# First product of the experts with weights stationary and tokens moving, rooms by rank, w1 and w3 in one array laid out by blocks

## The chip, the cores and the metric

The kernel runs on one core of one Trainium2 chip. The core has a matrix engine (TensorE: PE, with its weight loads shown apart as PEld), a vector engine (DVE), a scalar engine (ACT), a general engine (GpSimd: POOL) and SyncE (SP), which here only issues DMAs. The metric is device time in microseconds (us), the lower the better. All values are f32. Nearly every product is made of three: each operand is split into a rounded part "hi" and a rest "lo" (both of the type fp32r), and hi*hi + hi*lo + lo*hi is summed in PSUM.

## What is computed

One block of a network on 2048 tokens of width 1024: attention and a short convolution, then a mixture of experts, then a gated addition. The change lies in the experts (32 of them, in 4 groups of 8; every token goes to 2 experts of one group):

```python
def hier_moe(xn, w_group, b_group, w_router, b_router, w1, w3, w2):
    t, d = xn.shape                                        # 2048, 1024
    gl = (xn @ w_group).astype(jnp.float32) + b_group
    grp = jnp.argmax(gl, axis=-1)
    ...
    top_l, top_i = lax.top_k(el, TOP_K)                    # 2 of the 8 of the group
    wgt = (p_grp * jax.nn.softmax(top_l, axis=-1)).reshape(-1)
    eid = (grp[:, None] * EXPERTS_PER_GROUP + top_i).reshape(-1).astype(jnp.int32)
    ...
    def expert_block(args):
        xb, e = args
        hdn = jax.nn.silu(xb @ w1[e]) * (xb @ w3[e])       # 1024 -> 512
        return hdn @ w2[e]                                 # 512 -> 1024
```

The 4096 (token, expert) pairs are spread unevenly: by the reference's own routing of its inputs the 32 experts get, from the fullest to the emptiest, 177, 176, 171, 156, 152, 149, 149, 147, 146, 145, 145, 137, 137, 132, 132, 131, 129, 127, 120, 115, 113, 112, 112, 110, 108, 102, 102, 101, 94, 91, 91 and 87 rows.

## The kernel before

The program has four stages that follow each other: attention (`stage1`), convolution, gates and routing (`stage2`), the experts (`stage3`) and the gated addition (`stage4`). At the end of stage 2 `sort` ranks the experts by their rows, and writes for each rank the list of its tokens (`gidx` to gather, `sidx` to scatter) and the expert's number (`order`).

In `stage3` every expert has a room of fixed size: 192 rows for the 18 fullest (`NBIG`), 128 for the other 14. Rows over the room would go to a loop at the end (`overflow`); none is over here. The experts are taken in the order `proc`, in which large and small ones are mixed. For each one:

- `fetch` gathers the tokens' rows by an indirect DMA on POOL (part A: 128 rows, tile xgA; part B: 64 rows, xgB), two experts ahead. `prep` turns them on PE (lines L1008 and L1017) and splits them into xAh and xAl (ACT L1011, DVE L1012) and xB, in which hi and lo of the 64 rows stand side by side as 128 columns (L1019, L1020).
- `gemm1` multiplies with w1 and then w3: the tokens are stationary (128 x 128), the weights move with 512 columns at a time. For each of 8 pieces of the inner dimension part A takes three matmuls (`mm3`, L90 to L92), part B two (`mmB`, L1039 and L1040).
- Silu on ACT (L1073, L1077), the product of both on DVE (L1079) for A and on POOL (L1083) for B, where `fold` (L1045, L1046) has first added the hi rows to the lo rows.
- `turn_act` turns the result on PE (L1089, L1098) and splits it again into aAh, aAl and aB.
- `gemm2` multiplies with w2 (stationary: the turned result; moving: weights of 512 columns), copies to yA and yB and scatters them on POOL (L1106).

On PE the order is gemm1 of expert n, prep of n+1, gemm2 of n-1. Weights come in 384 chunks of 128 x 1024 f32 (512 KB): per expert four of w1, four of w3, four of w2. `chunk` takes the next one and asks `prefetch` for the one four further on. SP loads it into wraw (5 buffers), ACT makes whi (L79), and DVE or POOL make wlo (L80); whi and wlo have 7 buffers. POOL takes every fourth chunk, DVE the rest. Each engine works its instructions off in the order that the build's scheduler gave them. Results of matmuls go to 8 PSUM banks in turn.

The inner statements of the first product are:

```python
mm = self.mm3(pa, [(hi[:, k], lo[:, k])], [(ch[0][:, sl], ch[1][:, sl])], k, 8)
if xb is not None:
    mmB(pb, xb[:, k].rearrange("p s c -> p (s c)"), ch, sl, k == 0, k == 7)
```

## Time and profile before

| | us |
|---|---|
| median of 3 runs | 2657.95 |
| lowest and highest run | 2656.11, 2661.72 |
| the profiled execution, its own time | 2661.26 |
| its span (first to last instruction) | 2659.4 |
| expert stage in it, first transpose to last matmul of w2 (read off the timeline) | about 1627 to 2427 |

The page of the profile gives the busy time of each engine; the view by windows gives it for a stretch, with the granted clock of PE (1.00 is 2.4 GHz), the busy share of the DMA engines and what they moved. A matmul's record is longer than the time that it holds PE, since its end is modelled and the next one starts before it; so what one costs in a dense row is read from start to start. Names are those of the program: `acc<-whi,xAh` is a matmul into a PSUM bank, moving operand first, stationary operand behind it. In the view by line a row has the count, the busy time, the mean length of one and the idle time just before.

### The profile page before, as it was taken

The page shows a single profiled execution, that of the slowest core. Times are in us where ns is not written, and L with a number is a line of the kernel's source. Part 1 is how long each engine was busy: PE and PEld are TensorE (multiplying, and loading weights), DVE is VectorE, ACT ScalarE, POOL GpSimd, SP SyncE. Part 2 cuts the span into 40 slices and gives each one's busy share as a digit, 9 for nine tenths or more (in the row PEclk, how much of TensorE's full clock was granted, in tenths as well). Part 3 has the DMA queues.
Part 4 walks back from the last instruction along what each step waited for, and adds up shares of the span by engine and source line. Part 5 has one row for each costly group of instructions (what it writes and reads, how often), then busy time and mean ns, then how long its engine had stood idle before and what let it go on. Part 6 is the DMA issues. An engine that isn't in the chain of part 4 may idle for free.

```text
span 2659.4 us, 36515 instructions
## 1 busy us (share of the span) xinstructions
PE 2595.2 (98%) x13313; PEld 2184.5 (82%) x13313; DVE 1675.8 (63%) x2399; ACT 1341.6 (50%) x2025; POOL 841.0 (32%) x681
## 2 busy tenths in 40 slices
PE   7999999999999999999999998999999999998999
PEld 6898888878888888888888886888888888886887
DVE  7778867775444445444445446777777678775654
ACT  5666755564333323332333224766666666665322
POOL 2655465510000100010001003544554555542222
PEclk9999999999999999999999998999999999998999
DMA  5222311044335334533453346888989889987553
GB/s 185 72 68 60 110 48 41 9 129 137 102 128 189 103 95 143 170 102 95 137 170 103 95 151 210 307 309 295 315 304 313 302 314 309 312 309 258 207 187 103
DMA packets 349623, 465.11 MB, mean 175 GB/s; under 512 B 26240, under 2 KB 222080, under 8 KB 349440
## 3 DMA queue, kind: packets, MB, share of 16 engines
q1 hardware_dynamic: 314944, 388.35, 44.8%
q0 software_dynamic: 12096, 43.00, 4.3%
q10 hardware_dynamic: 22400, 31.41, 3.5%
q8 instruction: 105, 1.72, 0.3%
q14 instruction: 78, 0.64, 0.1%
HBM read 400.30 MB, written 62.39 MB: 174 GB/s over the span
## 4 chain that ended last, share of the span: by engine, by line
PE 84%; DVE 6%; DMA 4%; issue 3%; POOL 1%; ACT 1%; SPq 0%; another core or an unknown queue 0%; DVEq 0%; POOLq 0%; ACTq 0%
PE acc L90 22%; PE acc L92 22%; PE acc L91 22%; PE acc L1039 4%; PE acc L1040 4%; PE big L348 2%; PE big L380 2%; DMA h<-H 1%; DMA wraw<-w 1%; PE acc L393 1%; PE acc L394 1%; PE acc L1008 1%; PE acc L674 1%; PE acc L294 1%; POOL g L1362 1%
## 5 line engine op out<-in xcount | busy, mean ns | idle before, releaser
L80 DVE TENSOR_TENSOR wlo<-wraw,whi 128x1024 fp32r<-128x1024 f32 x464 | 694.5, 1509 | 478.4 <-ACT whi L79 465.3
L79 ACT CAST whi<-wraw 128x1024 fp32r<-128x1024 f32 x560 | 585.8, 1053 | 777.8 <-PE acc L91 375.6
L90 PE MATMUL acc<-nh,whi 128*128 128x512 f32 x896 | 349.7, 392 | 2.0 <-ACT nh L79 2.0
L91 PE MATMUL acc<-nl,whi 128*128 128x512 f32 x896 | 350.0, 391 | 0.0
L92 PE MATMUL acc<-nh,wlo 128*128 128x512 f32 x896 | 348.8, 389 | 0.0
L80 POOL TENSOR_TENSOR wlo<-wraw,whi 128x1024 fp32r<-128x1024 f32 x96 | 238.1, 2480 | 123.4 <-ACT whi L79 115.8
L599 POOL TENSOR_TENSOR sa<-sa,sc 128x512 f32<-128x512 f32 x32 | 41.3, 1290 | 538.3 <-DVE sc L598 493.2
L90 PE MATMUL acc<-whi,xAh 128*128 128x512 f32 x512 | 204.1, 399 | 0.4 <-ACT xAh L1011 0.4
L91 PE MATMUL acc<-wlo,xAh 128*128 128x512 f32 x512 | 200.1, 391 | 0.0
L92 PE MATMUL acc<-whi,xAl 128*128 128x512 f32 x512 | 200.0, 391 | 0.0
L90 PEld LDWEIGHTS acc<-nh,whi 128*128 128x128 f32 x896 | 168.1, 188 | 37.2 <-ACT nh L79 2.7
L92 PEld LDWEIGHTS acc<-nh,wlo 128*128 128x128 f32 x896 | 168.3, 188 | 34.5
L91 PEld LDWEIGHTS acc<-nl,whi 128*128 128x128 f32 x896 | 168.3, 188 | 33.4
L90 PE MATMUL acc<-wh,nh 128*128 128x512 f32 (+1 forms) x512 | 176.6, 346 | 0.3 <-ACT wh L79 0.2
L91 PE MATMUL acc<-wl,nh 128*128 128x256 f32 (+1 forms) x512 | 174.1, 341 | 2.1 <-DVE wl L80 2.1
L92 PE MATMUL acc<-wh,nl 128*128 128x256 f32 (+1 forms) x512 | 174.5, 342 | 0.0
L385 ACT CAST PTh<-big 128x640 fp32r<-128x640 f32 (+4 forms) x128 | 80.3, 628 | 85.7 <-PE big L380 84.3
L367 ACT ACTIVATE L<-L,mn 128x640 f32<-128x640 f32 (+4 forms) x128 | 98.4, 769 | 38.2 <-DVE mn L365 15.1
L90 PEld LDWEIGHTS acc<-whi,xAh 128*128 128x128 f32 x512 | 96.5, 189 | 20.8 <-ACT xAh L1011 1.0
L92 PEld LDWEIGHTS acc<-whi,xAl 128*128 128x128 f32 x512 | 96.3, 188 | 20.5 <-DVE xAl L1012 0.2
L1039 PE MATMUL acc<-whi,xB 128*128 128x512 f32 x288 | 112.9, 392 | 0.0
L1040 PE MATMUL acc<-wlo,xB 128*128 128x512 f32 x288 | 112.2, 390 | 0.0
(328 smaller groups left out, 5918.1 us busy)
## 6 DMA issues: line engine op xcount, KB each, us to landing
wraw<-w SPq DMA_DIRECT2D x384, 512.0 KB
wraw<-w_in SPq DMA_DIRECT2D x112, 512.0 KB
wraw<-w_o SPq DMA_DIRECT2D x32, 512.0 KB
y<-Y SPq DMA_DIRECT2D x32, 512.0 KB
xt<-x SPq DMA_DIRECT2D x16, 512.0 KB
xt<-NTd SPq DMA_DIRECT2D x16, 512.0 KB
nraw<-NTd ACTq DMA_DIRECT2D x32, 256.0 KB
wraw<-w_pa SPq DMA_DIRECT2D x32, 256.0 KB
```

Of the source, the lines that this page charges most:

```text
L79: (hi_eng or self.nc.scalar.copy)(hi, raw)
L80: (lo_eng or self.nc.vector).tensor_sub(lo, raw, hi.bitcast(F32))
L90: self.nc.tensor.matmul(ps, sh, mh, start=first, stop=False)
L91: self.nc.tensor.matmul(ps, sh, ml, start=False, stop=False)
L92: mm = self.nc.tensor.matmul(ps, sl, mh, start=False, stop=last)
L348: nc.tensor.matmul(big[:, 512 * c:512 * c + hi - lo], QT[g, t][:, s, h * 128:(h + 1) * 128], KT[0][:, h, ks:ks + hi - lo], start=(s == 0), ...
L367: nc.scalar.activation(L[:, :n], L[:, :n], AF.Exp, bias=mn, scale=-1.0, accum_out=sm)
L380: nc.tensor.transpose(pt[:, j * 128:(j + 1) * 128], L[:, j * 128:(j + 1) * 128], self.ident)
L385: nc.scalar.copy(hi, ptv)
L599: nc.gpsimd.tensor_tensor(sa, sa, sc, op=ALU.add)
L1039: nc.tensor.matmul(ps, st, ch[0][:, sl], start=first, stop=False)
L1040: nc.tensor.matmul(ps, st, ch[1][:, sl], start=False, stop=last)
```

## The change

- The first product is turned round: the weights are stationary (128 x 128 blocks), the tokens move. `x` holds, for each of the 8 pieces of the inner dimension, the hi of all c rows of the expert and behind it the lo of all c rows. The block whi is multiplied with 2c columns (hi and lo), the block wlo with the c columns of hi. ACT copies the second half of the bank (`zl`), DVE adds it to the first (`z0` or `z1`).
- The result comes out turned, so `turn_act` falls away. Silu is on ACT, the product on POOL, the split into `act` on ACT and DVE, once for each of the four 128-row blocks of the result. gemm2 stays as it is, with `act` as its stationary operand.
- Rooms are by rank, from 192 down to 96 rows in steps of 8 (sum 4312, before 18*192 + 14*128 = 5248). 17 of them are over 128. Gather, scatter, prep and gemm2 have c rows in place of 192 or 128.
- w1 and w3 are one array `w13`, laid out so that a chunk is one 128-column block of w1 or of w3 over the whole inner dimension; each partition reads 1024 values in one piece (before: two pieces of 512). There are still 8 chunks per expert for both, in turn w1, w3, w1, w3.
- POOL makes wlo of chunks 1, 4 and 6 of these 8, and of the last one of w2: 127 in all (before 96).
- In stage 1 four small tiles become one; two pads keep later tiles at their addresses.

```diff
-NBIG = 18
+
+ROOM = [192, 184, 176, 168, 160, 160, 152, 152, 152, 152, 152, 144, 144, 144, 136, 136,
+        136, 128, 128, 120, 120, 120, 120, 112, 112, 112, 104, 104, 104, 96, 96, 96]
+NBIG = sum(c > 128 for c in ROOM)
...
-                mn = att.tile([128, 1], F32, name="mn", bufs=4)
+                four = att.tile([128, 4], F32, name="four", bufs=4)
+                mn, mn0, sm, rs = (four[:, i:i + 1] for i in range(4))
...
-        nc.vector.tensor_scalar(f[:, 0:NBIG], cn[0:1, 0:NBIG], float(-CAP), 0.0, op0=ALU.add, op1=ALU.max)
-        nc.vector.tensor_scalar(f[:, NBIG:], cn[0:1, NBIG:], -128.0, 0.0, op0=ALU.add, op1=ALU.max)
+        nc.vector.tensor_sub(f, cn[0:1, :], self.c("room")[0:1])
+        nc.vector.tensor_scalar(f, f, 0.0, None, op0=ALU.max)
...
             if n < NE:
-                for w in (w1, w3):
-                    for k in range(4):
-                        self.add_chunk(lambda raw, w=w, i=proc[n], k=k: [(kv(raw), weights(w, i, k, 256))], nc.gpsimd if (k == 3 if n else w is w1 and k < 3) else None)
+                for q in range(8):
+                    self.add_chunk(lambda raw, i=proc[n], q=q: [(raw, weights(w13, i, q))], nc.gpsimd if q in (1, 4, 6) else None)
             if n > 0:
                 for k in range(4):
-                    self.add_chunk(lambda raw, i=proc[n - 1], k=k: [(raw.rearrange("p (k c) -> p k c", k=1), weights(w2, i, k, 128))],
-                                   nc.gpsimd if k == 3 and n < NE else None)
+                    self.add_chunk(lambda raw, i=proc[n - 1], k=k: [(raw, weights(w2, i, k))], nc.gpsimd if k == 3 and n < NE else None)
...
+            acts = [two.tile([128, 4, 2 * CAP], F32R, name=f"act{i}") for i in range(2)]
+            for t in acts:
+                nc.gpsimd.memset(t.bitcast(F32), 0.0)
...
+            def fetch(n):
+                if n < NE:
+                    i = proc[n]
+                    c = ROOM[i]
+                    ca = min(c, 128)
+                    G[n] = (gather(self.gidx[0][0:ca, i:i + 1], ca, "xgA"),
+                            gather(self.gidx[1][0:c - ca, i:i + 1], c - ca, "xgB") if c > ca else None)
+
+            def prep(n):
+
+                ga, gb = G.pop(n)
+                c = ROOM[proc[n]]
+                ca = min(c, 128)
+                x = two.tile([128, 8, 2 * CAP], F32R, name="x", bufs=2)
                 for hf in range(2):
                     tp = bank()
                     for k in range(4):
                         kk = 4 * hf + k
+                        nc.tensor.transpose(tp[:, 128 * k:128 * k + ca], ga[:, 128 * kk:128 * kk + 128], self.ident[0:ca, 0:ca])
+                    v = tp.rearrange("p (k c) -> p k c", k=4)[:, :, 0:ca]
+                    hi = x[:, 4 * hf:4 * hf + 4, 0:ca]
+                    nc.scalar.copy(hi, v)
+                    nc.vector.tensor_sub(x[:, 4 * hf:4 * hf + 4, c:c + ca], v, hi.bitcast(F32))
+                if gb is not None:
+                    cb = c - ca
+                    tp = bank()
+                    for k in range(8):
+                        nc.tensor.transpose(tp[:, 64 * k:64 * k + cb], gb[:, 128 * k:128 * k + 128], self.ident[0:cb, 0:cb])
+                    v = tp.rearrange("p (k c) -> p k c", k=8)[:, :, 0:cb]
+                    hi = x[:, :, ca:c]
+                    nc.scalar.copy(hi, v)
+                    nc.vector.tensor_sub(x[:, :, c + ca:2 * c], v, hi.bitcast(F32))
+                return x
+
+            def gemm1(n, x):
+
+                c = ROOM[proc[n]]
+                act = acts[n % 2]
+                for m in range(4):
+                    ps = []
+                    for w in range(2):
+                        hi, lo = self.chunk(4)
+                        p = bank()
+                        for k in range(8):
+                            sl = slice(128 * k, 128 * k + 128)
+                            nc.tensor.matmul(p[:, 0:2 * c], hi[:, sl], x[:, k, 0:2 * c], start=(k == 0), stop=False)
+                            nc.tensor.matmul(p[:, 0:c], lo[:, sl], x[:, k, 0:c], start=False, stop=(k == 7))
+                        z = two.tile([128, CAP], F32, name=f"z{w}", bufs=2)[:, 0:c]
+                        t = two.tile([128, CAP], F32, name="zl", bufs=2)[:, 0:c]
+                        nc.scalar.copy(t, p[:, c:2 * c])
+                        nc.vector.tensor_add(z, p[:, 0:c], t)
+                        if w == 0:
+                            nc.scalar.activation(z, z, AF.Silu)
+                        ps.append(z)
+                    nc.gpsimd.tensor_tensor(ps[0], ps[0], ps[1], op=ALU.mult)
+                    z, ca = ps[0], min(c, 128)
+                    hi = act[:, m, 0:c]
+                    self.turned = (nc.scalar.copy(hi, z),
+                                   nc.vector.tensor_sub(act[:, m, 256:256 + ca], z[:, 0:ca], hi[:, 0:ca].bitcast(F32)))
+                    if c > ca:
+                        nc.vector.tensor_sub(act[:, m, CAP:CAP + c - ca], z[:, ca:c], hi[:, ca:c].bitcast(F32))
+                return act
...
-                hi, lo, ab = act
+                c = ROOM[i]
+                ca = min(c, 128)
+                cb = c - ca
                 pa = [bank(), bank()]
-                pb = [bank(), bank()] if ab is not None else None
+                pb = [bank(), bank()] if cb else None
                 for k in range(4):
                     ch = self.chunk(ahead)
                     for hf in range(2):
                         sl = slice(512 * hf, 512 * hf + 512)
-                        self.last = self.mm3(pa[hf], [(hi[:, k], lo[:, k])], [(ch[0][:, sl], ch[1][:, sl])], k, 4)
-                        if ab is not None:
-                            mmB(pb[hf], ab[:, k].rearrange("p s c -> p (s c)"), ch, sl, k == 0, k == 3)
-                yA = two.tile([128, D], F32, name="yA" if n < NE - 1 else "xgA")
-                ev = [(nc.scalar.copy, nc.vector.tensor_copy)[hf](yA[:, 512 * hf:512 * hf + 512], pa[hf]) for hf in range(2)]
-                ev.append(scatter(self.sidx[0][:, i:i + 1], yA))
-                if ab is not None:
-                    yB = two.tile([64, D], F32, name="yB", bufs=1)
+                        self.last = self.mm3(pa[hf][0:ca], [(act[:, k, 0:ca], act[:, k, 256:256 + ca])], [(ch[0][:, sl], ch[1][:, sl])], k, 4)
+                        if cb:
+                            for q in range(2):
+                                nc.tensor.matmul(pb[hf], act[:, k, 128:256], ch[q][:, sl], start=(k == q == 0), stop=(k == 3 and q == 1))
...
-            ga, gb = G.pop(0)
-            x = (*prepA(ga), None)
+            x = prep(0)
             fetch(1)
-            act = None
+            acted = None
             for n in range(NE):
-                sAB = gemm1(x, None if n else gb)
+                act = gemm1(n, x)
                 if n + 1 < NE:
                     x = prep(n + 1)
                 fetch(n + 2)
-                if n == NE - 1:
-                    last = turn_act(*sAB)
-                if act:
-                    gemm2(n - 1, act)
-                if n < NE - 1:
-                    act = turn_act(*sAB)
-            ev = gemm2(NE - 1, last, 0)
+                if n:
+                    gemm2(n - 1, acted)
+                acted = act
+            ev = gemm2(NE - 1, acted, 0)
...
-        "w_group", "b_group", "w_router", "b_router", "w1", "w3", "w2", "g_ple", "w_ple_gate", "b_ple_gate", "w_ple_proj"]
+        "w_group", "b_group", "w_router", "b_router", "w2", "g_ple", "w_ple_gate", "b_ple_gate", "w_ple_proj"]
 
 
 def layout(inputs):
     arrays = {n: np.ascontiguousarray(inputs[n]) for n in _INS}
     arrays["rel_ext"] = np.ascontiguousarray(np.asarray(inputs["rel_bias"])[0][:, REL_INDEX])
     arrays["pT"] = np.ascontiguousarray(np.asarray(inputs["p"])[0, 0].T)
+
+    w13 = np.stack([np.asarray(inputs[n])[0].reshape(NE, 8, 128, 4, 128) for n in ("w1", "w3")])
+    arrays["w13"] = np.ascontiguousarray(w13.transpose(1, 4, 0, 3, 2, 5)).reshape(NE, 1024, 1024)
```

Three places show what this does to the engines' order. On PE, the end of one expert's second product and the start of the next first product; before (an expert with part B; sA is the result of Silu and product):

```order
L1040 MATMUL acc<-wlo,aB 128x512
L1089 MATMUL acc<-ident,sA 128x128 x4
L90 MATMUL acc<-whi,xAh 128x512
L91 MATMUL acc<-wlo,xAh 128x512
L92 MATMUL acc<-whi,xAl 128x512
L1039 MATMUL acc<-whi,xB 128x512
L1040 MATMUL acc<-wlo,xB 128x512
```

The five rows behind the transposes are one of 16 steps of an expert's first product (8 pieces, w1 and w3). Now, with a room of 152 rows behind one of 120:

```order
L94 MATMUL acc<-whi,act_14732 120x512
L95 MATMUL acc<-wlo,act_14732 120x512
L96 MATMUL acc<-whi,act_14732 120x512
L1053 MATMUL acc<-x,whi 128x304
L1054 MATMUL acc<-x,wlo 128x152
```

The transposes are gone, and a step is two matmuls, of which there are 64 per expert.

On POOL, around the second half of an expert's first product, before (Y is where results are scattered to):

```order
L999 DMA xgA_18391<-N2_68,gidx0_14924 128x1024
L1083 TENSOR_TENSOR sB_18298<-sB_18298,tB_18370 64x512
L80 TENSOR_TENSOR wlo_18460<-wraw_18457,whi_18459 128x1024
L1106 DMA Y_69<-yA_18473,sidx0_14926 16192x1024
```

The same place now:

```order
L84 TENSOR_TENSOR wlo_17715<-wraw_17712,whi_17714 128x1024
L1004 DMA xgA_17678<-N2_68,gidx0_14636 128x1024
L1004 DMA xgB_17680<-N2_68,gidx1_14637 24x1024
L1062 TENSOR_TENSOR z0_17617<-z0_17617,z1_17645 128x120
L84 TENSOR_TENSOR wlo_17775<-wraw_17772,whi_17774 128x1024
L1079 DMA Y_69<-yA_17760,sidx0_14638 16576x1024
L84 TENSOR_TENSOR wlo_17834<-wraw_17831,whi_17833 128x1024
L1079 DMA Y_69<-yB_17764,sidx1_14639 16576x1024
L1062 TENSOR_TENSOR z0_17795<-z0_17795,z1_17823 128x160
```

The product of w1's and w3's part (L1062), on which `act` waits, stands four times per expert on POOL, the last of them behind two gathers, the first of the next expert behind two scatters.

On DVE, before, a piece of a first product:

```order
L80 TENSOR_TENSOR wlo_18412<-wraw_18399,whi_18411 128x1024
L80 TENSOR_TENSOR wlo_18428<-wraw_18425,whi_18427 128x1024
L1079 TENSOR_TENSOR sA_18296<-sA_18296,acc_18303 128x512
L80 TENSOR_TENSOR wlo_18444<-wraw_18441,whi_18443 128x1024
L1046 TENSOR_TENSOR tB_18370<-acc_18304,tmp_18371 64x512
```

and now:

```order
L1066 TENSOR_TENSOR act0_14732<-z0_20274,act0_14732 128x128
L1068 TENSOR_TENSOR act0_14732<-z0_20274,act0_14732 128x24
L84 TENSOR_TENSOR wlo_20427<-wraw_20424,whi_20426 128x1024
L1058 TENSOR_TENSOR z1_20361<-acc_20344,zl_20362 128x152
L1030 TENSOR_TENSOR x_20369<-acc_20370,x_20369 128x4x112
L1030 TENSOR_TENSOR x_20369<-acc_20377,x_20369 128x4x112
L84 TENSOR_TENSOR wlo_20439<-wraw_20436,whi_20438 128x1024
L1066 TENSOR_TENSOR act0_14732<-z0_20333,act0_14732 128x128
```

Between the splits of weights there are now more and shorter instructions, some of which wait for POOL's product.

## Rows read from the trace of the kernel before

**Rows 1.** The page: busy time and share of engines; the chain that ended last.

```profile
PE 2595.2 (98%) x13313; PEld 2184.5 (82%) x13313; DVE 1675.8 (63%) x2399; ACT 1341.6 (50%) x2025; POOL 841.0 (32%) x681
...
PE 84%; DVE 6%; DMA 4%; issue 3%; POOL 1%; ACT 1%; SPq 0%; another core or an unknown queue 0%; DVEq 0%; POOLq 0%; ACTq 0%
```

**Rows 2.** View by windows: the expert stage's start, its body and its end.

```profile
core 0: us, PE busy (x) PEld busy (x) DVE busy (x) ACT busy (x) POOL busy (x), PEclk, DMA share, GB/s
1627.00:1700.00 73.00, 72.02 (x342) 58.53 (x343) 46.32 (x46) 44.96 (x58) 30.92 (x18) 0.96 0.76 251
1700.00:2400.00 700.00, 700.00 (x3343) 576.48 (x3342) 530.49 (x493) 475.48 (x594) 354.48 (x186) 1.00 0.89 308
2400.00:2427.00 27.00, 23.17 (x89) 17.74 (x88) 15.23 (x17) 12.10 (x16) 8.48 (x5) 0.87 0.90 310
```

**Rows 3.** PE's timeline (start, length, instruction): transposes and matmuls of the expert stage.

```profile
1671.56 1.04 PE L1008 MATMUL acc<-ident,xgA 128*128 128x128 f32 x8
...
2000.24 0.39 PE L1039 MATMUL acc<-whi,aB 128*128 128x512 f32 x1
...
2002.74 0.39 PE L1040 MATMUL acc<-wlo,aB 128*128 128x512 f32 x1
```

**Rows 4.** View by line and form, PE, expert stage.

```profile
L90 PE MATMUL acc<-whi,xAh 128*128 128x512 f32 x512 | 204.1, 399 | 0.4 <-ACT xAh L1011 0.4
...
L1039 PE MATMUL acc<-whi,xB 128*128 128x512 f32 x288 | 112.9, 392 | 0.0
...
L1089 PE MATMUL acc<-ident,sA 128*128 128x128 f32 x128 | 19.7, 277 | 0.5 <-DVE sA L1079 0.5
...
L1098 PE MATMUL acc<-ident,sB 64*128 64x64 f32 x72 | 8.2, 235 | 0.0
```

**Rows 5.** Timeline of PE and PEld in stage 1: fp32r matmuls of 128 columns.

```profile
332.72 0.31 PEld L348 LDWEIGHTS big<-KT,QT 128*128 128x128 f32 x2
332.84 0.33 PE L348 MATMUL big<-KT,QT 128*128 128x128 f32 x2
...
333.01 0.33 PE L91 MATMUL acc<-wl,nh 128*128 128x256 f32 x1
...
333.18 0.28 PE L92 MATMUL acc<-wh,nl 128*128 128x256 f32 x1
...
333.30 0.39 PE L90 MATMUL acc<-wh,nh 128*128 128x512 f32 x1
```

**Rows 6.** PE's timeline in stage 2: 16 matmuls of 36 columns.

```profile
1592.86 2.03 PE L674 MATMUL acc<-misc,nT 128*128 128x36 f32 x16
```

**Rows 7.** View by line and form, 1700 to 2400 us: ACT, DVE and POOL.

```profile
L79 ACT CAST whi<-wraw 128x1024 fp32r<-128x1024 f32 x339 | 354.3, 1053 | 207.9 <-DMA wraw<-w 119.2 <-PE acc L1039 59.2 <-PE acc L92 12.7
...
L1011 ACT CAST xAh<-acc 128x512 fp32r<-128x512 f32 x56 | 30.8, 587 | 0.4
...
L1101 ACT CAST aB<-acc 128x256 fp32r<-128x256 f32 x16 | 5.9, 370 | 0.3 <-PE acc L1098 0.3
...
L80 DVE TENSOR_TENSOR wlo<-wraw,whi 128x1024 fp32r<-128x1024 f32 x254 | 396.1, 1578 | 166.8 <-ACT whi L79 158.8 <-issue 4.3 <-PE acc L1040 1.6
L1012 DVE TENSOR_TENSOR xAl<-acc,xAh 128x512 fp32r<-128x512 f32 x57 | 37.0, 676 | 0.0
...
L1102 DVE TENSOR_TENSOR aB<-acc,aB 128x256 fp32r<-128x256 f32 x16 | 6.5, 409 | 0.4 <-ACT aB L1101 0.4
...
L80 POOL TENSOR_TENSOR wlo<-wraw,whi 128x1024 fp32r<-128x1024 f32 x85 | 210.2, 2473 | 103.0 <-ACT whi L79 101.5 <-issue 0.5
...
L1083 POOL TENSOR_TENSOR sB<-sB,tB 64x512 f32<-64x512 f32 x16 | 20.9, 1304 | 3.5 <-DVE tB L1046 3.3
```

**Rows 8.** Timelines of DVE and POOL: a split alone, and one beside POOL's.

```profile
2006.93 1.21 DVE L80 TENSOR_TENSOR wlo<-wraw,whi 128x1024 fp32r<-128x1024 f32 x1
...
2018.12 2.03 DVE L80 TENSOR_TENSOR wlo<-wraw,whi 128x1024 fp32r<-128x1024 f32 x1 [2.38 <-ACT whi L79]
...
2016.65 2.41 POOL L80 TENSOR_TENSOR wlo<-wraw,whi 128x1024 fp32r<-128x1024 f32 x1
```

More of the change, by code (lines that the diff above doesn't have):

```diff
@@ L39 @@
 _o = 0
-for _n, _w in (("iota", CAP), ("i4", 4), ("i8", 8), ("p", 1), ("key", NE), ("kcol", 1), ("eid", NE)):
+for _n, _w in (("iota", CAP), ("i4", 4), ("i8", 8), ("p", 1), ("key", NE), ("kcol", 1), ("eid", NE), ("room", NE)):
     CO[_n] = (_o, _o + _w)
@@ L62, in constants @@
     put("eid", (np.arange(128) % NE)[:, None])
+    put("room", np.array(ROOM))
     return c
@@ L112, in setup @@
         self.banks, self.nbank = [], 0
-        c.tile([128, 88], F32, name="pad")
+        c.tile([128, 24], F32, name="pad")
     def bank(self, dt=F32):
@@ L917, in overflow_rows @@
         nc.vector.tensor_copy(nb, ov)
-        a_, b_ = T("sa0", [NE]), T("sa1", [NE])
+        a_, b_ = (pool.tile([128, NE], F32, name="tmp", bufs=2) for _ in range(2))
         nc.vector.tensor_copy(a_, nb)
@@ L1022, in prepA @@
-            def prepA(ga):
-                hi = two.tile([128, 8, 128], F32R, name="xAh", bufs=2)
-                lo = two.tile([128, 8, 128], F32R, name="xAl", bufs=2)
-                turnA(ga, hi, lo)
-                return hi, lo
-            def prepB(gb):
-                xb = two.tile([128, 8, 2, 64], F32R, name="xB")
-                turnB(gb, xb)
-                return xb
-            def prep(e):
-                ga, gb = G.pop(e)
-                hi, lo = prepA(ga)
-                return hi, lo, prepB(gb) if gb is not None else None
@@ L1038, in mmB @@
-            def mmB(ps, st, ch, sl, first, last):
-                nc.tensor.matmul(ps, st, ch[0][:, sl], start=first, stop=False)
-                nc.tensor.matmul(ps, st, ch[1][:, sl], start=False, stop=last)
+                        nc.tensor.transpose(tp[:, 128 * k:128 * k + ca], ga[:, 128 * kk:128 * kk + 128], self.ident[0:ca, 0:ca])
+                    v = tp.rearrange("p (k c) -> p k c", k=4)[:, :, 0:ca]
+                    hi = x[:, 4 * hf:4 * hf + 4, 0:ca]
+                    nc.scalar.copy(hi, v)
@@ L1042, in fold @@
             def fold(out, ps):
+                cb = out.shape[0]
                 tmp = two.tile([64, 512], F32, name="tmp", bufs=2)
[L1045 to L1084 removed]
@@ L1086, in turn_act @@
[L1086 to L1103 removed]
+                nc.scalar.copy(tmp[0:cb], ps[64:64 + cb, :])
@@ L1105, in scatter @@
+                nc.vector.tensor_add(out, ps[0:cb, :], tmp[0:cb])
             def scatter(idx, y):
@@ L1145, in overflow @@
                         s, t = divmod(n, 16)
-                        oh = two.tile([128, 128], BF16, name="oho", bufs=2)
+                        oh = two.tile([128, 128], BF16, name="z0", bufs=2)
                         nc.vector.tensor_scalar(oh, tgt, over[s][:, t:t + 1], None, op0=ALU.is_equal)
@@ L1184, in overflow, with split_turned @@
-                    sA = two.tile([128, 512], F32, name="sA")
-                    nc.scalar.activation(sA, ph[0], AF.Silu)
-                    nc.vector.tensor_mul(sA, sA, ph[1])
-                    ahi, alo, _ = turn_act(sA, None)
+                    xs = two.tile([128, 2, 8, 128], F32R, name="x", bufs=2)
+                    def split_turned(src, dst, n):
+                        tp = bank()
+                        for k in range(4):
+                            nc.tensor.transpose(tp[:, 128 * k:128 * k + 128], src[:, 128 * (n + k):128 * (n + k) + 128], self.ident)
+                        v = tp.rearrange("p (k c) -> p k c", k=4)
+                        nc.scalar.copy(dst[:, 0, n:n + 4], v)
+                        nc.vector.tensor_sub(dst[:, 1, n:n + 4], v, dst[:, 0, n:n + 4].bitcast(F32))
@@ new lines, in overflow, with chunk @@
+                    for n in (0, 4):
+                        split_turned(xg, xs, n)
+                    def chunk(w, k):
+                        raw = two.tile([128, 1024], F32, name="xgA")
+                        nc.sync.dma_start(raw, w[bass.ds(e, 1)].rearrange("o r c -> (o r) c")[k * 128:(k + 1) * 128, :])
+                        wt = two.tile([128, 2, 1024], F32R, name="x", bufs=2)
+                        self.split(raw, wt[:, 0], wt[:, 1])
+                        return wt
+                    hid = two.tile([128, 512], F32, name="yB")
@@ new lines, in overflow @@
+                    for m in range(4):
+                        sl = slice(128 * m, 128 * m + 128)
+                        for w in range(2):
+                            wt = chunk(w13, 2 * m + w)
+                            ps = bank()
+                            for k in range(8):
+                                sk = slice(128 * k, 128 * k + 128)
+                                self.mm3(ps[:, 0:128], [(xs[:, 0, k], xs[:, 1, k])], [(wt[:, 0, sk], wt[:, 1, sk])], k, 8)
+                            if w == 0:
+                                nc.scalar.activation(hid[:, sl], ps[:, 0:128], AF.Silu)
+                            else:
+                                nc.vector.tensor_mul(hid[:, sl], hid[:, sl], ps[:, 0:128])
@@ L1378, in stage4 @@
             order.close()
-            two.tile([128, 48], F32, name="pad", bufs=1)
             add(todo[0], *ld[0][:2])
```

139 lines of the change are left out of this document (24 added, 115 removed).

## The prediction

> **What bounds the kernel now.** I read the page first [rows 1]: PE is busy 98% of the span, and the chain that ended last runs through PE for 84% of it. Then the windows [rows 2]: of the stage that the change touches, the body (1700 to 2400 us) has PE busy 700.00 of 700.00 us at clock 1.00; only its two ends have gaps. DVE is busy 76% there, ACT 68%, POOL 51%, the DMA engines 89% at 308 GB/s. So in this stage time is PE's instructions, and each of the others has room, DVE and the DMA engines least. The change is priced by what it does to PE first, and then by whether another engine grows past PE.
>
> A busy time does not tell what a matmul costs, because records overlap. In the timeline [rows 3] the twelfth instruction of a dense row of 512-column matmuls starts 2.50 us after the first (11 in between, of lines L90 to L92 and L1039, L1040): 0.2273 us each, while the view by form [rows 4] calls one 392 to 399 ns. I use 0.2273, or 0.444 ns per column.
>
> **First product, before.** Per piece and weight three matmuls for part A and two for part B where there is one: 32 x 48 = 1536 (512 of each of three kinds, [rows 4]) and 2 x 288 = 576, together 2112. At 0.2273 us: 480.1 us.
>
> **First product, now.** 64 pairs per expert, 2048 pairs: a wide matmul of 2c columns and a narrow one of c. If only columns counted, this were 3 x 4312 x 64 columns at 0.444 ns: 367 us, a gain of 113. The question is whether a short matmul is as cheap as its columns. Two places of the trace speak. In stage 1 two 128-column matmuls of fp32r start at 332.84, a 256-column one follows, the next 256-column one starts at 333.18 and the matmul behind it at 333.30 [rows 5]. A 256-column one thus takes 0.12 us; of the 0.34 from 332.84 to 333.18 that leaves 0.22 for the two short ones: 0.11 each, not the 0.057 of their columns. In stage 2 sixteen matmuls of 36 columns (plain f32, so a neighbour only) take 2.03 us, and the last record's tail of some 0.22 is not held time: 0.113 each [rows 6]. Both have a new stationary operand of 128 columns each time, as every matmul of the new first product has. So I take a floor of 0.111 us per matmul, which is about what 250 columns take.
>
> - Narrow: 96 to 192 columns, 43 to 85 ns by columns, so all lie under the floor: 2048 x 0.111 = 227.3 us.
> - Wide, the 19 rooms of 128 rows and more: 0.12 us at 256 columns and 0.418 ns for each one above; their rooms add to 2896, so 2.668 us x 64 = 170.7 us.
> - Wide, the 13 rooms under 128 (192 to 240 columns): between floor and 0.12, 0.115 x 13 x 64 = 95.7 us.
>
> Sum 493.7: **13.6 us more than before**, although nearly a quarter of the columns is gone (before: 2112 x 512). Ends: a floor of 0.107 gives -8 for the narrow ones, 0.12 gives +18.
>
> **What else PE gains.** The transposes of turn_act go: 128 of 128 columns and 72 of 64 columns [rows 4]. Eight of the first kind take 1.04 us with the last one's tail of 0.28 [rows 3], so 0.109 each: 14.0; the short ones I bound by 0.03 (columns) and 0.11 and take 0.07: 5.0. The second product has 16 matmuls of part B less, since 17 rooms instead of 18 are over 128: 3.6. Smaller preps: about 2. Together -24.6, so **PE's work falls by 11 us**, from 776 to about 765 in these sums.
>
> **Do the others stay below it?** By windows DVE is busy 592 us in the stage, ACT 532, POOL 394 [rows 2].
> - POOL: 31 more splits at 2.47 = +77; 128 products of c columns where 18 of 512 stood (1304 ns): at 2.3 ns a column and 0.13 us fixed, 56 - 23 = +33. About 504. [rows 7]
> - DVE: a split takes 1.21 us alone and 2.03 beside one of POOL's [rows 8], 1578 ns in the mean [rows 7]. With POOL splitting a third more often I take 1.77: 257 x 1.77 against 288 x 1.578 is no change. From 409 ns at 256 elements and 676 at 512 [rows 7] a small operation costs 142 ns and 1.04 per element: 256 additions (z0, z1) +72, some 190 act splits +50, the product, folds and turned splits gone -75, smaller preps -10. About 629 us, 82% of 765.
> - ACT: 370 ns at 256 and 587 at 512 [rows 7]: 256 copies (zl) +68, Silu and act casts +13, folds gone -21, with waits and Silu on SBUF uncertain up to +100. About 592 to 632.
> - DMA: the 384 loads of 512 KB stay 201.3 MB; gathered and scattered rows fall from 43.0 to 35.3 MB: 237 MB in 765 us is 309 GB/s, as now. A partition's 4 KB piece in place of two of 2 KB doesn't slow them.
>
> All lie under PE's 765, so none sets the time by itself. The chain ACT copy, DVE add, Silu, POOL product, split is long, but act is needed only after the next expert's whole first product (before, turn_act's split came just ahead of a second product too), so it hides behind 13 us or more of PE. Banks come free after copy and add, six banks behind PE. I allow 3 us for waits of the 32 experts.
>
> **Edits at nothing.** The one tile `four`, the pads and the room tables change no instruction of stage 1 that sets time and a few short ones of the sort; the memset of acts lies on POOL ahead of the first gather, in time when POOL waits for the routing. If that cover were gone it costs 2 x 1536 columns at POOL's rate above, at most 7 us once. The start of the stage now needs both gathers before PE begins (before, part B came in the middle of the first product), but two instead of four DVE splits stand beside them: -3 to +3, taken as 0.
>
> **Forecast.** -11 + 3 = -8 on the profiled execution's own 2661.3: 2653. That execution lies 3.3 above the median of the runs, so 2650. Its own range is 2635 to 2668, by the floor's two ends and the waits.
>
> **Rivals.**
>
> *The weight load hides better than in rows 5 (faster).* There, short ones followed each other; here every narrow one stands between wide ones, whose stream may cover the next load. A floor half way between the 0.06 of the mean narrow one's columns and 0.111, 0.085, saves 2048 x 0.026 = 53 on the narrow and about 15 on the small wide ones. PE would fall to 697, DVE's 629 plus its waits comes near, and I add 12 for that: 2590. For it: nothing in the trace has this alternation. Against: rows 5 is a mixed row too, and the 256-column one there hides nothing of its neighbours'. Chance 0.17.
>
> The Trainium skill (TensorE: Matmul & The Clock Gate, "Back-to-back issue gap") says that in a stream of weight loads and matmuls a matmul of 128 columns comes every 81 ns or so. By that figure, an estimate, the narrow ones would take 166 us and the kernel come out near 2580; the 0.111 us of rows 5, in fp32r, doesn't agree with it.
>
> *Short columns stream at half rate (slower).* 0.111 us for 128 columns is also just what half of 0.444 ns' rate gives, and no row has between 128 and 256 columns. Then narrow ones over 128 cost 0.888 ns a column (257 us together) and the small wide ones 161: sum 589, +109. 2661 + 109 - 25 + 3 - 3 = 2745. Against it: 192 columns would cost more than 256 do, and 36 columns cost as much as 128. Chance 0.06.
>
> *DVE and POOL set the pace of small experts (slower).* On POOL the product that DVE's and ACT's act splits wait for now stands behind splits of 2.4 us, gathers and scatters; DVE works in order, so wlo of the next chunk waits too. A 112-row expert is 20.8 us of PE (64 x 0.226, 24 x 0.2273, prep). DVE's eight splits, all beside POOL's at 2.03 [rows 8], are 16.2, its other work 5.0, four waits of 0.2 make 22.0. If so, 15 experts lose 1.2 each, +18, and with +3 at the start: 2671. It decides from where the mean DVE split passes some 1.9 us. For it: DVE's queue is already held up 167 us in the body, 159 of it by ACT's whi [rows 7]. Against: 1578 ns of mean now. Chance 0.12.
>
> *Rest:* rows over a room, or a clock that falls as short matmuls fill PE's array less; about 2720. Chance 0.03. Forecast: 0.62.
>
> **How the numbers follow.** A measurement here tells about 0.2%, 5.3 us, from no change. The forecast's own range lies on both sides: of its 0.62 I give 0.34 faster (below 2652.6), 0.17 same, 0.11 slower. With the rivals: faster 0.51, same 0.17, slower 0.32. The range takes in the faster rival down to 2585 and the DVE case with the floor's upper end, 2690; the half rate and the rest stay out.
>
> **What would show it.** Right: pairs of L1053 and L1054 that start 0.22 to 0.29 us apart with c, PE near 100% between 1700 and 2390, DVE's mean split near 1.77 us. Pairs of 0.19 in small rooms: the first rival; 0.30 or more in rooms of 112: the second; gaps on PE before L1053 with DVE's wlo as releaser, and DVE waiting for POOL's L1062: the third.

## The result and the profile after

The changed kernel takes 2768.93 us (median of 4 runs, 2754.33 to 2789.97) against 2657.15: 1.0423 times as long, 95% interval 1.0354 to 1.0493. Forecast was 2650, the range ended at 2690: wrong in sign and size. In what follows the time of a kernel is the median of all its runs, and a ratio leaves out a run that lies over 1.5% above the fastest of its kernel, as one of e1 and one of e5 does. The whole loss lies in the expert stage, first transpose to last matmul of w2: 903.3 us instead of 799.3; the span grew by 105.

The page's line of busy times and the window that answers to the middle one of [rows 2]:

```profile
PE 2643.0 (96%) x15073; PEld 2309.7 (84%) x15073; DVE 1778.7 (64%) x2699; ACT 1364.5 (49%) x2398; POOL 958.7 (35%) x822
...
core 0: us, PE busy (x) PEld busy (x) DVE busy (x) ACT busy (x) POOL busy (x), PEclk, DMA share, GB/s
1700.00:2400.00 700.00, 656.24 (x4245) 605.12 (x4245) 549.43 (x659) 430.08 (x805) 407.26 (x274) 0.90 0.78 262
```

No engine is full any more: PE has gaps of 44 us there, its granted clock is 0.90 instead of 1.00, and DVE, ACT and the DMA engines have time to spare. What PE waited for in the whole stage (us, times, longest):

```profile
PE acc L1096 <- DVE z L1058: 28.1, 12, 4.5
PE acc L1053 <- DVE x L1030: 17.5, 9, 4.2
PE acc L1053 <- DVE x L1039: 7.0, 3, 3.1
```

L1096 is part B of the second product, which waits for a PSUM bank that DVE's addition (L1058) has to read first; L1030 and L1039 are DVE's splits of the next expert's tokens. All are small instructions that stand late in DVE's queue. In the kernel before all waits of the stage came to 4.2 us.

The pairs themselves cost what was forecast. PE's timeline, first pairs of a 120-row room at full clock, then those of another room of 120 rows:

```profile
1950.26 0.33 PE L1053 MATMUL acc<-x,whi 128*128 128x240 f32 x1
1950.43 0.22 PE L1054 MATMUL acc<-x,wlo 128*128 128x120 f32 x1
1950.49 0.33 PE L1053 MATMUL acc<-x,whi 128*128 128x240 f32 x1
...
1809.51 0.52 PE L1053 MATMUL acc<-x,whi 128*128 128x240 f32 x1
1809.83 0.32 PE L1054 MATMUL acc<-x,wlo 128*128 128x120 f32 x1
1809.94 0.52 PE L1053 MATMUL acc<-x,whi 128*128 128x240 f32 x1
```

From pair to pair 0.23 us at the first place, 0.223 in the mean of all pairs of this width at full clock (forecast 0.226), but 0.43 at the second. The windows around 1800 us tell why:

```profile
1770.00:1795.00 25.00, 25.00 (x169) 23.77 (x168) 18.30 (x22) 14.39 (x26) 14.49 (x9) 1.00 0.81 248
1795.00:1800.00 5.00, 0.80 (x3) 0.38 (x3) 4.54 (x6) 3.83 (x9) 3.94 (x4) 0.93 0.56 179
1800.00:1833.00 33.00, 33.00 (x151) 31.94 (x151) 21.54 (x26) 16.26 (x31) 15.15 (x11) 0.50 0.74 253
1833.00:1860.00 27.00, 27.00 (x179) 25.20 (x178) 16.94 (x23) 16.60 (x30) 12.45 (x9) 0.99 0.62 207
```

PE idles 4.2 us, then is busy without a break for 33 us at clock 0.50 (1.2 GHz): the whole first product of this expert and the start of the second product of the expert before it. With 512-column matmuls running, the clock is back. Behind the start of the stage the trace has 13 such stretches, each behind a gap of 2.1 to 4.5 us: ten last 3.4 to 6.8 us, three last 27 to 34 us. The three long ones stand at first products of rooms of 120, 120 and 104 rows.

**Where 104 us went.** With the gaps and half of the busy time at half clock taken off, a stage's length is its work at full clock (all three summed from the trace of each kernel's profiled run):

| | stage | gaps | busy at half clock | left: work at full clock |
|---|---|---|---|---|
| before | 799.3 | 4.2 | 11.1 | 789.6 |
| after | 903.3 | 57.2 | 147.3 | 772.4 |

PE's work fell by 17 us. Gaps added 53 and the clock (147.3 - 11.1) / 2 = 68.

**How a gap comes about.** Timelines of POOL, ACT, DVE and PE ahead of that gap (in brackets: idle before, and what ended it):

```profile
1781.07 2.41 POOL L84 TENSOR_TENSOR wlo<-wraw,whi 128x1024 fp32r<-128x1024 f32 x1
1785.36 0.90 POOL L1079 DMA_INDIRECT Y<-yB,sidx  x1 [1.88 <-DVE z L1058]
1786.28 0.55 POOL L1062 TENSOR_TENSOR z<-z,z 128x168 f32<-128x168 f32 x1
...
1790.34 2.41 POOL L84 TENSOR_TENSOR wlo<-wraw,whi 128x1024 fp32r<-128x1024 f32 x1
...
1795.02 2.36 POOL L84 TENSOR_TENSOR wlo<-wraw,whi 128x1024 fp32r<-128x1024 f32 x1
...
1786.86 0.33 ACT L1065 CAST act<-z 128x168 fp32r<-128x168 f32 x1 [6.04 <-POOL z L1062]
...
1787.23 0.29 DVE L1066 TENSOR_TENSOR act<-z,act 128x128 fp32r<-128x128 f32 x1 [2.41 <-ACT act L1065]
...
1790.77 2.12 DVE L1066 TENSOR_TENSOR act<-z,act 128x128 fp32r<-128x128 f32 x1 [0.69 <-ACT act L1065]
...
1795.46 2.07 DVE L1066 TENSOR_TENSOR act<-z,act 128x128 fp32r<-128x128 f32 x1 [0.85 <-ACT act L1065]
...
1798.95 1.21 DVE L1030 TENSOR_TENSOR x<-acc,x 128x480 fp32r<-128x480 f32 x2
...
1799.64 0.57 PE L1053 MATMUL acc<-x,whi 128*128 128x240 f32 x1 [4.20 <-DVE x L1030]
```

Two things hold DVE. POOL's product (L1062) stands behind a split and a scatter; ACT stands still for 6.04 us, then DVE for 2.41. And the act split (the subtraction that makes act's lo, L1066), 0.29 us by itself, takes 2.12 and 2.07 when it starts just behind the start of POOL's next split, ending 0.15 us after that ends. So it is in the whole stage: of the act splits of 128 columns the 50 that start while a POOL split runs take 2.07 to 2.50 us, the 24 with POOL idle 0.27 to 0.29. By line, 1700 to 2400 us, in this kernel and then in the experiment without POOL splits:

```profile
L84 DVE TENSOR_TENSOR wlo<-wraw,whi 128x1024 fp32r<-128x1024 f32 x196 | 291.9, 1490 | 67.7 <-ACT whi L83 65.9 <-PE acc L96 1.6
L1066 DVE TENSOR_TENSOR act<-z,act 128x128 fp32r<-128x128 f32 (+3 forms) x100 | 149.8, 1498 | 52.9 <-ACT act L1065 52.9
L1058 DVE TENSOR_TENSOR z<-acc,zl 128x152 f32<-128x152 f32 (+9 forms) x197 | 55.3, 288 | 28.0 <-ACT zl L1057 27.2
```

```profile
L84 DVE TENSOR_TENSOR wlo<-wraw,whi 128x1024 fp32r<-128x1024 f32 x315 | 381.6, 1221 | 116.2 <-ACT whi L83 110.2 <-issue 3.6 <-PE acc L1053 1.0
L1058 DVE TENSOR_TENSOR z<-acc,zl 128x152 f32<-128x152 f32 (+10 forms) x211 | 61.0, 289 | 0.0
...
L1066 DVE TENSOR_TENSOR act<-z,act 128x128 fp32r<-128x128 f32 (+4 forms) x107 | 30.0, 281 | 69.9 <-ACT act L1065 69.8
```

The act split falls from 1498 to 281 ns. The addition L1058, with one operand from PSUM, takes 288 and 289 in both. The Trainium skill (SBUF — State Buffer, "Who interferes with whom") says that VectorE and GpSimd hold a shared port pair by an exclusive lock for a whole instruction, and that a DVE instruction with two SBUF inputs is among those that block. These rows agree.

### The profile page after: what moved, and what is told of

The parts are those of the page before. It is cut to its first block, busy times and chain, and to the rows that moved or that the text cites. A ratio compares the mean times of both kernels' runs of the same rounds, so it can differ in the third digit from the quotient of the medians.

```text
span 2764.4 us, 41365 instructions
## 1 busy us (share of the span) xinstructions
PE 2643.0 (96%) x15073; PEld 2309.7 (84%) x15073; DVE 1778.7 (64%) x2699; ACT 1364.5 (49%) x2398; POOL 958.7 (35%) x822
## 3 DMA queue, kind: packets, MB, share of 16 engines
q1 hardware_dynamic: 282176, 388.35, 43.1%
## 5 line engine op out<-in xcount | busy, mean ns | idle before, releaser
L84 DVE TENSOR_TENSOR wlo<-wraw,whi 128x1024 fp32r<-128x1024 f32 x433 | 630.6, 1457 | 397.3 <-ACT whi L83 391.0
L1053 PE MATMUL acc<-x,whi 128*128 128x304 f32 (+12 forms) x2048 | 537.9, 355 | 25.9 <-DVE x L1030 17.5
L1054 PE MATMUL acc<-x,wlo 128*128 128x152 f32 (+12 forms) x2048 | 487.8, 240 | 0.4 <-POOL wlo L84 0.4
L1053 PEld LDWEIGHTS acc<-x,whi 128*128 128x128 f32 x2048 | 416.6, 204 | 32.2 <-DVE x L1030 21.9
L1054 PEld LDWEIGHTS acc<-x,wlo 128*128 128x128 f32 x2048 | 420.9, 206 | 1.2 <-POOL wlo L84 0.5
L84 POOL TENSOR_TENSOR wlo<-wraw,whi 128x1024 fp32r<-128x1024 f32 x127 | 307.5, 2422 | 83.4 <-ACT whi L83 73.7
L1066 DVE TENSOR_TENSOR act<-z,act 128x128 fp32r<-128x128 f32 (+4 forms) x128 | 180.3, 1409 | 66.9 <-ACT act L1065 66.8
L1062 POOL TENSOR_TENSOR z<-z,z 128x152 f32<-128x152 f32 (+12 forms) x128 | 81.9, 640 | 194.5 <-DVE z L1058 144.5
L1065 ACT CAST act<-z 128x152 fp32r<-128x152 f32 (+12 forms) x128 | 39.0, 305 | 167.2 <-POOL z L1062 166.9
L370 ACT ACTIVATE L<-L,four 128x640 f32<-128x640 f32 (+4 forms) x128 | 98.4, 769 | 39.0 <-DVE four L363 15.7
```

The lines of the kernel that those rows point to most:

```text
L84: (lo_eng or self.nc.vector).tensor_sub(lo, raw, hi.bitcast(F32))
L370: nc.scalar.activation(L[:, :n], L[:, :n], AF.Exp, bias=mn, scale=-1.0, accum_out=sm)
L1053: nc.tensor.matmul(p[:, 0:2 * c], hi[:, sl], x[:, k, 0:2 * c], start=(k == 0), stop=False)
L1054: nc.tensor.matmul(p[:, 0:c], lo[:, sl], x[:, k, 0:c], start=False, stop=(k == 7))
L1062: nc.gpsimd.tensor_tensor(ps[0], ps[0], ps[1], op=ALU.mult)
L1066: nc.vector.tensor_sub(act[:, m, 256:256 + ca], z[:, 0:ca], hi[:, 0:ca].bitcast(F32)))
```

## The experiments

Theory: POOL's queue (its splits, its scatters) and its splits' hold on DVE make PE's gaps; the clock falls behind a gap and short matmuls keep it down. Rivals: DVE has too much work; or the clock is independent of the matmuls' length. Each ratio is against the kernel before on the same chip, in brackets the 95% interval. The last three columns are those of the table above (us in the expert stage), from one profiled run of each kernel; that run took 13 us more than the median in e1, 7 more in e2 and 16 less in e10.

| kernel | us | ratio | gaps | busy at half clock | work at full clock |
|---|---|---|---|---|---|
| e1 no POOL splits | 2720.75 | 1.0203 [1.0183, 1.0224] | 29.7 | 140.6 | 771.6 |
| e2 product on DVE | 2740.89 | 1.0271 [1.0230, 1.0311] | 47.9 | 113.2 | 773.4 |
| e3 POOL splits as before | 2774.54 | 1.0420 [1.0383, 1.0458] | 54.2 | 167.2 | 770.9 |
| e4 wide lo | 2738.71 | 1.0290 [1.0267, 1.0312] | 64.5 | 65.1 | 776.1 |
| e5 act's subtraction on POOL, no splits there | 2767.39 | 1.0354 [1.0286, 1.0423] | 41.8 | 177.5 | 770.2 |
| e6 whole tail on POOL, no splits there | 2645.48 | 0.9945 [0.9924, 0.9965] | 4.2 | 10.6 | 768.4 |
| e7 as e6, wide lo | 2645.54 | 0.9945 [0.9926, 0.9963] | 4.2 | 12.6 | 770.0 |
| e8 as e1, wide lo | 2704.34 | 1.0156 [1.0127, 1.0184] | 36.4 | 48.5 | 775.0 |
| e9 old rooms | 2751.71 | 1.0337 [1.0307, 1.0367] | 38.6 | 56.2 | 820.5 |
| e10 tail on POOL, splits kept | 2741.75 | 1.0324 [1.0286, 1.0362] | 43.1 | 76.7 | 774.9 |
| e11 no POOL splits, product on DVE | 2644.37 | 0.9944 [0.9927, 0.9961] | 4.5 | 10.6 | 768.4 |
| e12 kernel before, no POOL splits | 2653.86 | 0.9975 [0.9964, 0.9987] | 0.2 | 5.1 | 789.1 |

**e1.** POOL makes no wlo.

```diff
-... nc.gpsimd if q in (1, 4, 6) else None)
-... nc.gpsimd if k == 3 and n < NE else None)
+... None)
```

> One part undone and gone further: POOL makes no wlo at all, DVE makes all 384; POOL keeps the product and the gathers and scatters. Theory (DVE is held by POOL's splits: in the changed kernel the act split of 128 columns takes 1.65 us where 0.28 is its own time, and POOL's product, on which ACT and DVE wait, stands behind splits of 2.4 us; PE gets gaps of 2 to 4.5 us from that, and the clock falls to 1.2 GHz behind each): DVE's splits fall to 1.21, the act split to 0.28, PE's gaps of 57 us in the stage to under 15, half-clock time in the stage from 159 us to under 40, time 2640 to 2670. Rival (DVE simply has too much work; 127 more splits make it the bound): 384 x 1.21 + 200 of other work = 665 us spread unevenly, gaps in the experts with small rooms grow, time 2770 or more.

The rival falls: DVE with all splits is not slower but 48 us faster than the changed kernel. The theory's number was missed too: gaps halved, but 29.7 us stayed, and with four stretches of 27 to 31 us the time at half clock hardly fell. What is left shows in POOL's, ACT's and DVE's timeline:

```profile
2243.42 0.86 POOL L1079 DMA_INDIRECT Y<-yB,sidx  x1 [8.44 <-DMA Y<-yA,sidx]
2244.31 0.49 POOL L1062 TENSOR_TENSOR z<-z,z 128x144 f32<-128x144 f32 x1
...
2244.84 0.31 ACT L1065 CAST act<-z 128x144 fp32r<-128x144 f32 x1 [10.37 <-POOL z L1062]
...
2245.18 0.29 DVE L1066 TENSOR_TENSOR act<-z,act 128x128 fp32r<-128x128 f32 x1 [9.42 <-ACT act L1065]
```

The scatter of part B waits for that of part A to land, and POOL's product behind it makes ACT stand for 10.37 us and DVE for 9.42.

**e2.** The product on DVE, POOL's splits kept.

```diff
-nc.gpsimd.tensor_tensor(ps[0], ps[0], ps[1], op=ALU.mult)
+nc.vector.tensor_tensor(ps[0], ps[0], ps[1], op=ALU.mult)
```

> One wait taken away: the product z0*z1 on DVE instead of POOL, POOL's splits stay as in the changed kernel. If what hurts is that the product stands in POOL's queue behind splits and scatters: ACT's wait of 167 us for it goes, PE's gaps fall by half or more, about 2700. If what hurts is that DVE's own SBUF instructions stand still beside a POOL split: the 128 products on DVE are held as the act splits are (1.2 to 2.4 us instead of 0.3), DVE gets 38 to 150 us more, time 2770 to 2820.

Between both, by time and by DVE's rows (1700 to 2400 us):

```profile
L1066 DVE TENSOR_TENSOR act<-z,act 128x128 fp32r<-128x128 f32 (+3 forms) x104 | 94.6, 910 | 5.4 <-ACT act L1065 5.2
L1062 DVE TENSOR_TENSOR z<-z,z 128x152 f32<-128x152 f32 (+9 forms) x103 | 94.0, 913 | 6.2
```

The product, on DVE, took 913 ns in the mean (0.29 where POOL has no splits, in e11), the act split 910. One cause is gone, the hold by POOL's splits is left.

**e3.** `if q in (1, 4, 6)` becomes `if q in (3, 7)`.

> One part undone: POOL makes wlo of two of the eight w13 chunks (the fourth and the eighth) and of the last of w2, about 95 in all as in the kernel before, instead of 127. Theory (POOL's splits hold DVE): between the changed kernel and the one without POOL splits, 2700 to 2740. Rival (DVE has too much work): 32 more DVE splits, slower than the changed kernel, 2780 to 2810.

No difference from the changed kernel, so neither side was right. With 32 splits less on POOL the product still stands in one queue with the other 95 splits and the scatters.

**e4.** The clock by itself.

```diff
+cl = 2 * c if c <= 128 else c
-nc.tensor.matmul(p[:, 0:c], lo[:, sl], x[:, k, 0:c], ...)
+nc.tensor.matmul(p[:, 0:cl], lo[:, sl], x[:, k, 0:cl], ...)
```

> The clock by itself: in the 15 rooms of up to 128 rows the narrow matmul moves the 2c columns as well (192 to 256 instead of 96 to 128), which adds the product of the two rests; nothing else changes, so the gaps' causes stay. At full clock a pair then costs 0.23 to 0.24 us instead of 0.224: up to 10 us more. Theory (a gap lets the clock fall, and short matmuls behind it keep it at 1.2 GHz for a whole first product: three stretches of 27 to 34 us): the long stretches shrink to 7 to 10 us, gaps stay at 50 to 60 us, time 2735 to 2755. Rival (the length of the half-clock stretches has nothing to do with the length of the matmuls): the long stretches stay, time 2775 to 2785.

As the theory said. Gaps got no shorter (64.5 us in sum), yet the long stretches are gone, busy time at half clock falls from 147 to 65 us and the kernel by 30. One expert with 120 rows has a gap ahead of its first product in both, 4.0 us (at 1999.4 us) in the changed kernel and 4.7 us (at 1989.0 us) here. Windows of the changed kernel, then of this one:

```profile
2000.00:2020.00 20.00, 16.60 (x81) 16.60 (x81) 16.23 (x20) 11.65 (x21) 10.45 (x8) 0.60 0.88 303
2020.00:2040.00 20.00, 20.00 (x99) 18.49 (x99) 10.55 (x13) 10.14 (x19) 9.71 (x7) 0.71 0.56 169
```

```profile
1980.00:2000.00 20.00, 15.34 (x95) 13.65 (x94) 16.00 (x21) 13.87 (x26) 11.76 (x10) 0.91 0.75 259
2000.00:2020.00 20.00, 19.61 (x140) 17.68 (x139) 17.16 (x21) 12.07 (x27) 14.03 (x10) 1.00 0.86 300
2020.00:2040.00 20.00, 20.00 (x151) 19.36 (x150) 15.93 (x19) 14.20 (x26) 13.04 (x8) 1.00 0.69 245
```

The other runs say the same. In the changed kernel, e1, e2, e3, e5 and e10 all 19 falls of the clock at first products of rooms of 96 to 120 rows last 27 to 34 us; in e4 and e8, with the wide lo, the seven at such rooms last 3.4 to 6.8. The wider matmuls cost next to nothing: a pair with two of 224 columns takes 0.22 us, 0.11 each, as much as 224 and 112 did.

**e5.** As e1, and the subtractions for act's lo (L1066, L1068) on POOL.

> No splits of weights on POOL; product and the subtraction for act's lo on POOL, the rounding to act's hi stays on ACT. So ACT alone still waits for POOL's product, DVE no more directly. If the engine that matters is ACT (it makes every whi in order, and a whi behind a waiting rounding is late for all): ACT waits 100 us and more for POOL as in the run without POOL splits, PE's gaps stay above 20 us, 2690 to 2720. If it is DVE's own wait for act's hi: gaps go, 2645 to 2660.

What ACT and DVE waited for longest (1700 to 2390 us):

```profile
ACT act L1065 <- POOL z L1062: 140.6, 63, 9.9
```

```profile
DVE wlo L84 <- ACT whi L83: 232.6, 135, 9.9
```

It is ACT: DVE no longer waits for act's hi, but ACT still waited 140.6 us for POOL's product, and DVE's wait for whi, made on ACT behind it, rose to 232.6 us. The time, 2767, lies 47 us above what was expected for this case. Five long stretches at half clock stand in the trace where e1 has four; that is 31 of the 37 us that e5 has more there.

**e6.** As e5, and the rounding to act's hi on POOL, so that the whole tail of the first product (product, rounding, subtraction) is there. Against the changed kernel, beside e1's edit:

```diff
-self.turned = (nc.scalar.copy(hi, z), nc.vector.tensor_sub(act...
+self.turned = (nc.gpsimd.tensor_copy(hi, z), nc.gpsimd.tensor_sub(act...
```

> No splits of weights on POOL, and the whole tail of the first product on POOL: product, rounding to act's hi, subtraction for its lo (before: rounding on ACT, subtraction on DVE). So ACT and DVE wait for POOL no more; POOL alone waits for its scatters. Theory (in the run without POOL splits ACT still waited 140 us in the stage for POOL's product, which stood in POOL's queue behind a scatter of part B that waits for the scatter of part A, 8.4 us once; from there come PE's last gaps of 29 us and the half clock behind them): PE's gaps fall under 12 us, half clock under 40 us in the stage, time 2640 to 2660. Rival (the gaps come from DVE's work, or act now comes late from POOL): gaps of 25 us or more stay, 2700 or more.

The theory holds. Its window is that of [rows 2] again:

```profile
1700.00:2400.00 700.00, 700.00 (x5055) 652.90 (x5054) 553.92 (x721) 491.18 (x838) 438.66 (x504) 1.00 0.89 310
```

**e7** and **e8.** The edit of e4 on top of e6, and on top of e1.

> The kernel with the tail on POOL, and in rooms of up to 128 rows the narrow matmuls move 2c columns as well. If the gaps are gone already: 0 to 10 us slower than that kernel (a pair 0.23 to 0.24 in place of 0.224). If gaps and long stretches at half clock are left in it: faster than it by about half of those stretches.

> The kernel without POOL splits (2720.8 us, four stretches of 27 to 31 us at half clock, PE's gaps 29 us), with the wider narrow matmuls of rooms of up to 128 rows. Theory (short matmuls behind a gap hold the clock down): the four long stretches shrink to 3 to 7 us, about 45 us less and up to 7 us more, 2675 to 2690. Rival: 2720 or more.

e7 equals e6: without gaps the width doesn't matter. In e8 the four long stretches went, as expected, but gaps grew from 29.7 to 36.4 us, and 2704 came of it instead of 2675 to 2690. In its profiled run the stage also began later, at 1634.9 us instead of 1625.2.

**e9.** `ROOM = [192] * 18 + [128] * 14`.

> One part undone: rooms of 192 (18) and 128 (14) rows as in the kernel before, all else as in the changed kernel. By the pairs' times read in the changed kernel's trace (0.285 us at 192 rows, 0.231 at 128) the first product is 18 x 64 x 0.285 + 14 x 64 x 0.231 = 535 us at full clock, 42 more than with rooms by rank; no wide matmul is under 256 columns, so if short matmuls hold the clock down the long stretches go (about -45): 2760 to 2775, and gaps rarer, since PE has more work per expert. If rooms don't bear on the clock: 2800 or more.

Work at full clock is 48 us more (42 of it by the pairs' prices), and still the kernel is 17 us faster than the changed one, and 8 faster than the expected range: gaps 38.6 us instead of 57.2, half clock 56.2 instead of 147.3, no long stretch. (The intervals of the two ratios overlap a little.) So of the rooms' saving nothing arrived in the changed kernel. The 820.5 us are also 31 more than the kernel before needs: with rooms of the old sizes the turned product costs PE time, and what it gains comes from the rooms by rank.

**e10.** As e6, with POOL's splits kept.

> The whole tail (product, rounding, subtraction) on POOL, and POOL's 127 splits of weights as in the changed kernel. POOL then has 127 x 2.42 = 307 us of splits, about 230 of tail (439 us of POOL in 700 in the run with the tail alone, half of it gathers and scatters) and 200 of gathers and scatters: 740 in a stage of 780, in one queue in which splits stand behind scatters that wait. If the waits of ACT and DVE for the tail are the whole cause, 2645 to 2665. If a wlo from POOL that comes late stops PE just as well: PE waits for POOL's wlo, which it did for under 2 us in the changed kernel, and the time is 2720 or more. I expect the second.

The number fits, the reason given for it doesn't: PE waited for no wlo of POOL's, but 28.2 us for DVE's additions, DVE's splits took 1854 ns each and waited 139.6 us for whi, and ACT waited 112 us for weights to arrive.

**e11.** The edits of e1 and e2 together: POOL has gathers and scatters only.

> No splits of weights on POOL and the product on DVE: POOL has gathers and scatters only, so nothing that ACT or DVE waits for stands in its queue. ACT still waits for the product and DVE for act's hi, but on engines that wait for no scatter. Theory (the waits come from POOL's queue, first its splits, then its scatter of part B behind that of part A): ACT's wait for the product falls from 140 us to under 60, PE's gaps to under 15, 2650 to 2680; DVE's work is 38 us more than in the run without POOL splits. Rival (the chain over three engines in order is too tight in itself, or DVE has too much work): 2700 or more.

Faster than expected, and the simplest version that beats both kernels. Its window, and what ACT waited for in the changed kernel, in e1 and here:

```profile
1700.00:2400.00 700.00, 700.00 (x5052) 652.73 (x5051) 599.12 (x1014) 514.89 (x955) 113.94 (x87) 1.00 0.90 310
```

```profile
ACT act L1065 <- POOL z L1062: 139.8, 77, 6.6
```

```profile
ACT act L1065 <- POOL z L1062: 132.3, 66, 10.4
```

```profile
ACT act L1065 <- DVE z L1062: 26.9, 28, 1.7
```

DVE is busiest of all kernels here (599 of 700 us), and PE has no gap in these 700 us: it was never a matter of DVE's sum. Nor is it the order of the work, which is planned anew with each edit: in the traces of e1, e6 and e11 PE's matmuls of the stage stand in one and the same order, and so do the 402 instructions of DVE that read PSUM, there and in the changed kernel.

**e12.** A control: the kernel before without POOL splits.

> A control: the kernel before with all 384 splits on DVE, none on POOL, and nothing else. In the kernel before PE is busy 700 of 700 us and DVE's splits have cover, so if the 0.56% that the new first product gains without POOL splits comes from PE's work, this kernel stays within 0.3% of the one before: 2650 to 2667 (DVE's busy time in the stage falls or stays, 384 x 1.21 against 288 x 1.58). If the gain came from freeing DVE and POOL as such, this one is at about 2645 too. If the kernel before needs POOL's help, it is slower, 2675 or more.

0.25% faster, mostly from the stage's end, where the gaps and half clock near 2410 us are gone. So of the 0.56% of e11 nearly half comes with POOL's splits gone; the rest, 0.31%, is what the turned product with its rooms is worth. The stage itself is 13.8 us shorter than in e12 (778.1 against 791.9), but e11 takes 4 us longer from the stage's end to the end of the program (235.0 against 230.9); why was not followed up.

## Right and wrong, step by step

- **The price of short matmuls: right.** Pairs of 192 and 96 columns take 0.223 us and of 384 and 192 0.285, as the floor of 0.111 and [rows 5, 6] gave (0.226 and 0.285). Neither the faster rival (0.085) nor half rate happened.
- **PE's work: right in sign, undersized.** Forecast 11 us less; by the table 17 less in the changed kernel, 21 in e6 and e11.
- **"All lie under PE's 765, so none sets the time by itself": true and beside the point.** In e11 DVE is busy for 651 us and ACT for 562 of a stage of 778. The step that failed is the next one: that the long chain hides behind 13 us of PE, at 3 us for all waits. act is indeed not needed early (PE waited 0.5 us for it in the changed kernel); but ACT and DVE work in order, and while they wait for POOL's product, the next weights' whi, the next tokens' split and the additions that free PSUM banks wait behind. The gaps came to 57 us. The prediction had named that queue in its third rival, and priced it at 1.2 us for 15 small experts, 18 in all: the mechanism was there, at a third of the gaps' size and without the clock. It looked for wlo as what comes late, which stopped PE for 2 us in all; the additions and the splits of tokens did for 53.
- **A DVE price taken from the wrong row.** The act split was priced by instructions that read PSUM [rows 7], 0.28 us. It reads SBUF alone, like the weights' split of [rows 8], which shows the hold: 2.03 us beside POOL's. So it took 1.5 us in the mean, and the point from which the rival decides, a mean weight split of 1.9 us, was the wrong gauge: that stayed at 1.49.
- **The clock: missed.** It was given 0.03, as an effect of short matmuls by themselves. By themselves they don't: e6 has as many, and 1.00 in its window. Each fall stands behind a gap, and behind a gap the first products of small rooms ran at 1.2 GHz nearly from end to end. 68 us, the largest single term.
- **The start of the stage, gathers, loads: right.** It began at 1630.2 instead of 1627.6 us, and without gaps (e11) the DMA engines moved 310 GB/s where 308 were moved before.

Two things stay open: why one gap more falls at a small room in e5 than in e1, and whether POOL could keep some splits if the order of its queue were set by hand.

## What to carry to other kernels

A step that is taken off the critical engine can still stop it: ask of each instruction that waits what stands behind it on its own engine, and put a chain whose result is wanted late on an engine on which nothing urgent queues. Price a vector instruction by a row with its operands in the same memories, beside the same neighbours. And where a change makes matmuls short, a gap that cost its own length before may cost a whole product's time at half clock, so the gaps have to go first.
